# A weighted sum of two experts: the first load takes one token of each partition instead of two

## The chip, the cores and the metric

The kernel runs on one NeuronCore of a Trainium2 chip. The metric is the device time of one execution in microseconds (us). Before the change the median of three runs is 239.23 us (239.12 to 240.39). Times of single instructions and transfers come from one profiled execution of the same kernel.

## The reference

For each of 16 x 1024 tokens there are two expert outputs of 512 float32 values, and two weights. The result is their weighted sum:

```python
batch, seq, hidden, n_experts, k = 16, 1024, 512, 8, 2
expert_outputs: (batch, seq, k, hidden) float32
combine_weights: (batch, seq, k) float32

weights = combine_weights[..., np.newaxis]
return np.sum(expert_outputs * weights, axis=2).astype(np.float32)
```

67.1 MB are read as expert outputs, 0.13 MB as weights, and 33.6 MB are written. No matrix product is in it.

## The kernel before

**Tokens on partitions.** The 16,384 tokens are spread over 128 partitions, 128 tokens each. A token is 4 KB of input (two halves of 512 float32) and 2 KB of output. Of each partition's tokens the first 120 (`main`) are contiguous in memory; the last 8 come from a second region. `rows` (line 40) gives the view for tokens `t` to `t + c` of every partition, so a load of `c` tokens reads 128 contiguous stretches of `c` times 4 KB.

**Tiles and rooms.** A tile is 12 tokens per partition (6 MB in, 3 MB out). There are ten of them and a last one of 8 tokens (`TILES`, line 30). SBUF holds `et`, four rooms of 12 tokens; tile `g` lies in room `g % 4`. All the weights lie in `wt`, 256 values per partition.

**Loads.** `load` (line 68, its transfer on line 71) is issued on SP's queue. Five loads open the kernel (lines 109 to 112): `FIRST` has 2, 10, 12, 12 and 12 tokens, so that the first two fill tile 0 and the others tiles 1 to 3. The very first has the option `max_dma_last_dim`, k x h x 4 = 4096, which cuts its 8 KB rows into 4 KB pieces. No other load has it.

**What else opens.** ACT's queue first gets an 8 KB store of zeros from `zt` into 16 rows of the output (line 104), which later stores overwrite, and then the weights in two transfers (lines 105 and 106, through line 74): 120 tokens' worth, 960 B for each partition, then the last 8, 64 B each. ACT then loads its function table with a small activation (line 107).

**Tiles 0 to 8** (`WHOLE`) are computed on VectorE alone: one multiplication of the room by the weights, broadcast along the 512 values (line 83), and one addition of the two halves (line 90), which puts the result into the room's own first half. **Tile 9** takes 12 ScalarE activations with a scale (line 95) and 12 VectorE instructions that multiply and add (line 96). **Tile 10** (`MIXED`) has its first halves scaled by ScalarE (line 87), its second by VectorE (line 89), and then the addition.

**Stores and reloads** (lines 114 to 124). After each tile its result is stored (line 121), through ACT's queue for tiles 0 to 7. Tiles 8 and 9 are stored together, and tile 10 alone, through SP's. The load of tile `g + 4` is issued on SP after the store of tile `g`, whose room it fills; it waits until that store has landed. The order is written by hand (`manual_schedule`), so each queue runs in the order of these lines.

Of the kernel before, what the change touches and what calls it, by code (L numbers as in the profile page):

```python
# [1 line left out]

# [4 lines left out]


@with_exitstack
def kernel(  # L10
    ctx: ExitStack,
    tc: tile.TileContext,
    expert_outputs: bass.AP,
    combine_weights: bass.AP,
    out: bass.AP,
):

    nc = tc.nc
    b, s, k, h = expert_outputs.shape
    assert k == 2
    n = b * s
    P = nc.NUM_PARTITIONS
    per = n // P
    assert per * P == n

    ROOM, ROOMS = 12, 4
    TILES = [12, 12, 12, 12, 12, 12, 12, 12, 12, 12, 8]  # L30
    FIRST = [2, 10, 12, 12, 12]
    STORES = [[0], [1], [2], [3], [4], [5], [6], [7], [8, 9], [10]]
    WHOLE = [0, 1, 2, 3, 4, 5, 6, 7, 8]
    MIXED = [10]
    LAST = 8
    assert sum(TILES) == per and [g for st in STORES for g in st] == list(range(len(TILES)))
    main = per - LAST
    starts = [sum(TILES[:g]) for g in range(len(TILES))]

    def rows(x):  # L40

        first = x[0 : P * main, :].rearrange("(p t) f -> p t f", p=P)
        second = x[P * main : n, :].rearrange("(p t) f -> p t f", p=P)
        return lambda t, c: first[:, t : t + c, :] if t < main else second[:, t - main : t - main + c, :]

    flat = out.rearrange("b s h -> (b s) h")
    eo = rows(expert_outputs.rearrange("b s k h -> (b s) (k h)"))
    cw = rows(combine_weights.rearrange("b s k -> (b s) k"))
    o = rows(flat)

    dt = mybir.dt.float32
    mult = mybir.AluOpType.mult
    add = mybir.AluOpType.add
    copy = mybir.ActivationFunctionType.Copy

    pool = ctx.enter_context(tc.tile_pool(name="all", bufs=1))
    et = pool.tile([P, ROOMS * ROOM, k * h], dt)
    halves = et.rearrange("p j (k h) -> p (j k) h", k=k)
    wt = pool.tile([P, per * k], dt)
    wk = wt.rearrange("p (t k) -> p t k", k=k)  # L60
    zt = pool.tile([16, 128], dt)
    warm = pool.tile([P, 1], dt)

    def place(t):
        g = max(g for g in range(len(TILES)) if starts[g] <= t)
        return g % ROOMS * ROOM + t - starts[g]

    def load(t, c, **kw):
        at = place(t)
        assert place(t + c - 1) == at + c - 1  # L70
        nc.sync.dma_start(out=et[:, at : at + c], in_=eo(t, c), **kw)  # L71

    def weights(q, t, c):
        q.dma_start(out=wk[:, t : t + c, :], in_=cw(t, c))

    def combine(g, base):
        at, c, t0 = g % ROOMS * ROOM, TILES[g], starts[g]
        if g in WHOLE or g in MIXED:
            room = halves[:, k * at : k * (at + c), :]
            x0, x1 = et[:, at : at + c, 0:h], et[:, at : at + c, h : 2 * h]  # L80
            if g in WHOLE:
                wb = wt[:, k * t0 : k * (t0 + c)].unsqueeze(2).to_broadcast([P, k * c, h])
                nc.vector.tensor_tensor(out=room, in0=room, in1=wb, op=mult)  # L83
            else:
                for i in range(c):
                    x = et[:, at + i, 0:h]
                    nc.scalar.activation(out=x, in_=x, func=copy, scale=wt[:, k * (t0 + i) : k * (t0 + i) + 1])  # L87
                w1 = wk[:, t0 : t0 + c, 1:2].to_broadcast([P, c, h])
                nc.vector.tensor_tensor(out=x1, in0=x1, in1=w1, op=mult)  # L89
            nc.vector.tensor_tensor(out=halves[:, base : base + c, :], in0=x0, in1=x1, op=add)  # L90
            return
        for i in range(c):
            t = k * (t0 + i)
            x0, x1 = halves[:, k * (at + i), :], halves[:, k * (at + i) + 1, :]
            nc.scalar.activation(out=x0, in_=x0, func=copy, scale=wt[:, t : t + 1])  # L95
            nc.vector.scalar_tensor_tensor(  # L96
                out=halves[:, base + i, :], in0=x1, scalar=wt[:, t + 1 : t + 2], in1=x0, op0=mult, op1=add
            )

    with tc.manual_schedule():  # L100
        nc.vector.memset(zt, 0.0)  # L101

        ahead = flat[0 : P * main, :].rearrange("(q t) h -> q (t h)", q=16)
        nc.scalar.dma_start(out=ahead[:, 0:128], in_=zt)  # L104
        weights(nc.scalar, 0, main)
        weights(nc.scalar, main, per - main)
        nc.scalar.activation(out=warm, in_=nc.const_aps.tensor(1.0, (P, 1), dt), func=copy)  # L107

        t = 0
        for i, c in enumerate(FIRST):  # L110
            load(t, c, **({"max_dma_last_dim": k * h * 4} if i == 0 else {}))
            t += c
        assert t == sum(TILES[:ROOMS])
        for j, st in enumerate(STORES):
            base, c = st[0] % ROOMS * ROOM * k, 0
            for g in st:
                combine(g, base + c)
                c += TILES[g]
            assert c <= k * ROOM
            q = nc.sync if j in (8, 9) else nc.scalar  # L120
            q.dma_start(out=o(starts[st[0]], c), in_=halves[:, base : base + c, :])
            for g in st:
                if g + ROOMS < len(TILES):
                    load(starts[g + ROOMS], TILES[g + ROOMS])


# [1 line left out]
_INS = ['expert_outputs', 'combine_weights']  # L128
_OUTS = [((16, 1024, 512), 'float32')]


# [23 lines left out]
```

## Time and profile before

| What | us |
|---|---|
| Median of three runs | 239.23 |
| Lowest, highest | 239.12, 240.39 |
| The profiled execution | 239.0 |
| Its span in the profile | 237.2 |
| VectorE busy in it | 192.3 |
| ScalarE busy in it | 14.0 |
| A multiplication of a whole tile (line 83) | 12.96 |
| An addition of a whole tile (line 90) | 6.56 |

The span runs from the first instruction to the last, and the time around it (1.8 us) is not in the trace. All times within the trace count from the start of the span. SP, ACT and DVE in the rows are SyncE, ScalarE and VectorE; a `q` behind a name (SPq) means the engine's own instruction queue, where transfers are issued and semaphores awaited. `q1` and `q10` are DMA queues; each is served by the same 16 DMA engines. A packet in these rows is one piece that a DMA engine moves. A transfer's landing is the moment at which its semaphore is complete. The page counts 3616 packets, 100.80 MB, and a mean of 425 GB/s over the span.

A row of the waits reads: engine and line that waited, what it waited for, us in total, times, longest wait. A row of DMA issues reads: destination, source, queue, number of such transfers, KB each, median us from issue to landing.

### The profile page before, as it was taken

The page shows a single profiled execution, that of the slowest core. Times are in us where ns is not written, and L with a number is a line of the kernel's source. Part 1 is how long each engine was busy: PE and PEld are TensorE (multiplying, and loading weights), DVE is VectorE, ACT ScalarE, POOL GpSimd, SP SyncE. Part 2 cuts the span into 40 slices and gives each one's busy share as a digit, 9 for nine tenths or more (in the row PEclk, how much of TensorE's full clock was granted, in tenths as well). Part 3 has the DMA queues.
Part 4 walks back from the last instruction along what each step waited for, and adds up shares of the span by engine and source line. Part 5 has one row for each costly group of instructions (what it writes and reads, how often), then busy time and mean ns, then how long its engine had stood idle before and what let it go on. Part 6 is the DMA issues. An engine that isn't in the chain of part 4 may idle for free.

```text
span 237.2 us, 155 instructions
## 1 busy us (share of the span) xinstructions
DVE 192.3 (81%) x33; ACT 14.0 (6%) x22; POOL 0.2 (0%) x4
## 2 busy tenths in 40 slices
DVE  0009999999999999999999879969996998673820
ACT  2000000000000000000000000000000000743400
POOL 0000000000000000000000000000000000000000
DMA  7999999989899999999797999999998979999997
GB/s 289 452 475 398 398 506 423 398 348 514 352 443 423 439 464 464 398 398 522 340 530 340 456 414 448 464 464 398 398 506 356 522 340 464 453 409 442 398 442 309
DMA packets 3616, 100.80 MB, mean 425 GB/s; under 512 B 528, under 2 KB 672, under 8 KB 928
## 3 DMA queue, kind: packets, MB, share of 16 engines
q1 hardware_dynamic: 2144, 75.50, 74.1%
q10 hardware_dynamic: 1472, 25.31, 24.8%
HBM read 67.24 MB, written 33.56 MB: 425 GB/s over the span
## 4 chain that ended last, share of the span: by engine, by line
DMA 58%; DVE 35%; ACT 2%; ACTq 0%; issue 0%; DVEq 0%; SPq 0%
DMA out_dram<-et 29%; DMA et<-in_expert_outputs_dram 22%; DVE et L83 22%; DVE et L90 13%; DMA wt<-in_combine_weights_dram 7%; ACT et L87 2%; ACTq L150 0%; ACTq L104 0%; DVE zt L101 0%; DVEq L83 0%; SPq L71 0%; ACTq L87 0%
## 5 line engine op out<-in xcount | busy, mean ns | idle before, releaser
L83 DVE TENSOR_TENSOR et<-et,wt 128x12288 f32<-128x12288 f32 x9 | 116.6, 12955 | 24.1 <-DMA wt<-in_combine_weights_dram 17.2
L90 DVE TENSOR_TENSOR et<-et 128x6144 f32<-128x6144 f32 (+1 forms) x10 | 63.4, 6345 | 0.9 <-ACT et L87 0.6
L95 ACT ACTIVATE et<-et,wt 128x512 f32<-128x512 f32 x12 | 7.5, 708 | 199.1 <-DMA et<-in_expert_outputs_dram 199.1
L96 DVE SCALAR_TENSOR_TENSOR et<-et,wt 128x512 f32<-128x512 f32 x12 | 8.0, 747 | 3.1 <-ACT et L95 3.1
L89 DVE TENSOR_TENSOR et<-et,wt 128x4096 f32<-128x4096 f32 x1 | 4.4, 4426 | 5.4 <-DMA et<-in_expert_outputs_dram 5.4
L87 ACT ACTIVATE et<-et,wt 128x512 f32<-128x512 f32 x8 | 5.0, 709 | 6.7 <-DMA et<-in_expert_outputs_dram 6.7
L107 ACT ACT_TABLE_LOAD x1 | 1.3, 1283 | 2.4 <-issue 2.4
L101 DVE MEMSET zt<- 16x128 f32 x1 | 0.2, 165 | 0.8 <-PEq L139 0.8
L107 ACT ACTIVATE warm<-const-float32-1.0 128x1 f32<-128x1 f32 x1 | 0.2, 202 | 0.0
L139 POOL MEMSET const-bfloat16-1.0<- 128x1 bf16 x1 | 0.1, 101 | 0.0
L139 POOL MEMSET const-uint8-127<- 128x1 uint8 x1 | 0.1, 101 | 0.0
L139 POOL MEMSET const-float32-0.0<- 128x1 f32 x1 | 0.1, 98 | 0.2 <-issue 0.2
L139 POOL MEMSET const-float32-1.0<- 128x1 f32 x1 | 0.1, 98 | 0.0
## 6 DMA issues: line engine op xcount, KB each, us to landing
et<-in_expert_outputs_dram SPq DMA_DIRECT2D x9, 6144.0 KB, 29.9
out_dram<-et ACTq DMA_DIRECT2D x8, 3072.0 KB, 33.9
out_dram<-et SPq DMA_DIRECT2D x1, 6144.0 KB, 19.8
et<-in_expert_outputs_dram SPq DMA_DIRECT2D x1, 5120.0 KB, 16.7
et<-in_expert_outputs_dram SPq DMA_DIRECT2D x1, 4096.0 KB, 22.4
out_dram<-et SPq DMA_DIRECT2D x1, 2048.0 KB, 9.8
et<-in_expert_outputs_dram SPq DMA_DIRECT2D x1, 1024.0 KB, 4.6
wt<-in_combine_weights_dram ACTq DMA_DIRECT2D x1, 120.0 KB, 16.7
```

Source lines behind the costliest of these rows:

```text
L83: nc.vector.tensor_tensor(out=room, in0=room, in1=wb, op=mult)
L87: nc.scalar.activation(out=x, in_=x, func=copy, scale=wt[:, k * (t0 + i) : k * (t0 + i) + 1])
L89: nc.vector.tensor_tensor(out=x1, in0=x1, in1=w1, op=mult)
L90: nc.vector.tensor_tensor(out=halves[:, base : base + c, :], in0=x0, in1=x1, op=add)
L95: nc.scalar.activation(out=x0, in_=x0, func=copy, scale=wt[:, t : t + 1])
L96: nc.vector.scalar_tensor_tensor(out=halves[:, base + i, :], in0=x1, scalar=wt[:, t + 1 : t + 2], in1=x0, op0=mult, op1=add)
L101: nc.vector.memset(zt, 0.0)
L107: nc.scalar.activation(out=warm, in_=nc.const_aps.tensor(1.0, (P, 1), dt), func=copy)
L139: nc = _bacc.Bacc("TRN2", target_bir_lowering=False, num_devices=1)
```

## The change

The sizes of the opening loads go from 2, 10, 12, 12, 12 to 1, 11, 12, 12, 12 tokens per partition. The first DMA then loads one token per partition, a 4 KB row, and keeps its option; the second loads the other 11 tokens of tile 0, 44 KB rows. Besides, the rooms' size becomes a list with one entry for each room, all 12, and a room's place is looked up in a list of starts. The places come out as before, and so do all other instructions.

```diff
-    ROOM, ROOMS = 12, 4
+    ROOM = [12, 12, 12, 12]
+    ROOMS = len(ROOM)
+    SITE = [sum(ROOM[:i]) for i in range(ROOMS)]
     TILES = [12, 12, 12, 12, 12, 12, 12, 12, 12, 12, 8]
-    FIRST = [2, 10, 12, 12, 12]
+    FIRST = [1, 11, 12, 12, 12]
...
+    assert all(c <= ROOM[g % ROOMS] for g, c in enumerate(TILES))
...
-    et = pool.tile([P, ROOMS * ROOM, k * h], dt)
+    et = pool.tile([P, sum(ROOM), k * h], dt)
...
     def place(t):
         g = max(g for g in range(len(TILES)) if starts[g] <= t)
-        return g % ROOMS * ROOM + t - starts[g]
+        return SITE[g % ROOMS] + t - starts[g]
...
     def combine(g, base):
-        at, c, t0 = g % ROOMS * ROOM, TILES[g], starts[g]
+        at, c, t0 = SITE[g % ROOMS], TILES[g], starts[g]
...
-            base, c = st[0] % ROOMS * ROOM * k, 0
+            base, c = SITE[st[0] % ROOMS] * k, 0
...
-            assert c <= k * ROOM
+            assert c <= k * ROOM[st[0] % ROOMS]
```

## The prediction

> **What bounds the kernel now.** I read the page's DMA rows first, then the chain of waits, then the DMA queues in short windows. The page gives VectorE 81% of the span, but the queue rows decide:
>
> ```profile
> q1 hardware_dynamic: 2144, 75.50, 74.1%
> q10 hardware_dynamic: 1472, 25.31, 24.8%
> ```
>
> These are packets, MB and share of the 16 DMA engines' span; q1 carries what SP issues, q10 what ACT issues. Together 98.9%: the engines idle 1.1% of 237.2 us, 2.6 us. A window from 1.8 to 236.0 us gives
>
> ```profile
> q1 hardware_dynamic: 2141, 75.50, 75.0%
> q10 hardware_dynamic: 1472, 25.31, 25.2%
> ```
>
> 100.2%, so the idle time is 1.8 us before the first packet and about 1 us behind the last. The kernel moves its 100.8 MB without a gap. The chain of waits (start, duration, what) says where work begins and ends:
>
> ```profile
> 1.42 16.66 DMA wt<-in_combine_weights_dram
> ...
> 18.17 12.97 DVE et L83
> ...
> 76.67 30.88 DMA out_dram<-et
> ...
> 107.62 29.94 DMA et<-in_expert_outputs_dram
> ...
> 222.21 4.43 DVE et L90
> ```
>
> VectorE starts at 18.17, when the weights land. From there the chain goes through long DMA pieces: 29.94 us for a 6 MB load and 30.88 us for a 3 MB store. These are queueing: a load and a store together (9.44 MB) take 21.75 us, the spacing of load issues (64.09, 85.89, 107.62), which is 434 GB/s. VectorE needs only 12.96 + 6.56 = 19.5 us for a tile, so from the sixth tile on it waits for loads:
>
> ```profile
> DVE et L83 <- DMA wt<-in_combine_weights_dram: 17.2, 1, 17.2
> DVE et L83 <- DMA et<-in_expert_outputs_dram: 6.9, 4, 2.2
> ```
>
> **The start, packet by packet.** The DMA issue rows (KB, us from issue to landing):
>
> ```profile
> et<-in_expert_outputs_dram SPq DMA_DIRECT2D x1, 5120.0 KB, 16.7
> et<-in_expert_outputs_dram SPq DMA_DIRECT2D x1, 1024.0 KB, 4.6
> wt<-in_combine_weights_dram ACTq DMA_DIRECT2D x1, 120.0 KB, 16.7
> wt<-in_combine_weights_dram ACTq DMA_DIRECT2D x1, 8.0 KB, 30.8
> ```
>
> The first load is issued at 0.73 and lands at 5.3. The second, issued at 1.21, lands at 17.9. The 120 KB of weights, issued at 1.42, land at 18.08. The packet count says how rows travel: q1's 2144 packets are 256 of 4 KB (the first load), 13 x 128 for the other 11 loads and two stores, one per partition, and 16 closing ones for each of 14 transfers (224). So the second load is 128 packets of 40 KB, 8 per engine; the weights are 8 per engine of 960 B. Two short windows, 6 to 7 and 14 to 15 us, show them alternating, one for one:
>
> ```profile
> q1 hardware_dynamic: 16, 0.66, 151.4%
> q10 hardware_dynamic: 16, 0.02, 4.4%
> ```
>
> The same two lines come from both windows. Each weights packet waits for one big packet, so the eight of them end with the second load's eighth. The small weights transfer repeats it: it lands at 32.7 with the third load (32.5), 8 rounds in 14.6 us, 1.83 us a round.
>
> **The change part by part.**
>
> *Issue.* SP's first issue takes 0.43 us (256 packets), the others 0.33. With 128 packets I take 0.33: the second load's issue moves from 1.21 to about 1.1. Whether the first packet comes sooner is not shown; bounds 0 and -0.1 us; I take -0.05. All later issues in the opening move by as much and queue behind loads in transit. The fifth load, issued at 5.34 when the first landed (4.94 us of SP issues from 0.73 on), is issued at about 4.0; it has two loads ahead of it: nothing.
>
> *Transfer of tile 0.* Bytes are equal. A window from 3.2 to 3.6 us shows 40 packets of 4 KB, 0.16 MB, so 0.16 us per packet and engine. Ten tokens in 40 KB are one round of (17.9 - 5.3)/8 = 1.57 us, 0.157 per token. 128 packets dropped are 8 per engine: 8 x 0.16 = 1.28 us less, and eight rounds longer by 0.157 are 1.26 more: -0.02 us. The first packets are slower: 1 MB took from 1.8 to 4.8, 3.0 us against 16 x 0.16 = 2.6. If those 0.4 us go with the packets, half is saved (-0.2); if they belong to starting, nothing. I take -0.05, since later small packets show no such cost.
>
> *Does the second load follow in time?* The first load's packets now end at 4.8 - 1.3 = 3.5 us. The second was ready at 4.8 at the latest and is issued 0.1 earlier, so at worst the engines idle 4.7 - 3.5 = 1.2 us. SP's first load needed 1.1 us from issue to packet; that gives 1.1 + 1.1 = 2.2, no gap. I take 0, the row of the same queue, and keep 0 to +1.2.
>
> *The weights.* The page's 8 KB store of zt goes ahead of them on ACT's queue. Its packets move in the window 3.6 to 4.4, between 4 KB packets where a turn costs 0.16 us. Now only 44 KB packets are there from 3.5 on, so its data, its closing packet, and then the weights, each wait for one: a round of 11 x 0.157 = 1.73 us. The eight weights packets then need more rounds than the second load has left and end beside the third, at 1.83 us a round. If zt still slips in before 3.5, the weights lose one round; behind the first big packet, two; behind the second, three. Bounds: 0 rounds and 4 (7.3 us). I take two, +3.7 us: the weights land near 21.8 and VectorE starts there instead of at 18.17. Queued behind that wait on VectorE are all tiles, and on ACT the stores of their results.
>
> *Who pays for that?* Nobody, as long as a packet is queued. While the first store is late by 3.7 us, q1 has loads to move (four loads, 24 MB, 58 us at 434 GB/s), and moves them without sharing. Store 0 is issued at 37.75 + 3.7 = 41.4, lands near 67.8, and load 4 is issued then instead of at 64.09. Load 3 landed at 5.34 + 66.9 = 72.2; it now gains the two 24 KB packets that did not come between, 2 x 0.91 = 1.8 us (24 KB at 434/16 GB/s), and lands near 70.4: load 4 is still queued in time. From then on loads land some 1.8 us earlier, so the 6.9 us of waits in the row above shrink and VectorE has made up its 3.7 us by about tile 7 (21.75 - 19.5 = 2.2 us a tile). The cover is the DMA backlog; without it the whole 3.7 us would show. At the end the last store, issued at 226.7, lands 9.8 us later although 2 MB need 4.8: it stands behind the 6 MB store on q1, with some 5 us to spare less its own start. Nothing at the end is late.
>
> Sum: -0.05 - 0.02 - 0.05 + 0 + 0 = -0.1 us, on a profiled 239.0 (span 237.2 and 1.8 around it). The three runs have a median of 239.23, 0.2 above, so I forecast 239.1.
>
> **The rivals.**
>
> *A gap behind the short first load* (above): up to +1.2 us, middle 0.6, so 239.8 and at most 240.4. For it: zt's store needed over 2.5 us from issue (1.01) to its first packets. Against it: SP's own 1.1 us, and 4 KB packets followed at once by big ones. The Trainium skill, "DMA: Bandwidth & Descriptors", section "Rules for kernel authors", asks for at least 1 MiB per DMA, and its "Anatomy of one DMA" gives a fixed 2.0 us and bytes at 436 GB/s for transfers issued from GpSimd; the halved first load lasts 1.2 us by that, which would leave 0.8 us uncovered, an estimate from that page, 239.9. The trace shows no transfer from GpSimd, so it can neither agree nor disagree here.
>
> *The weights ride with the third load altogether*: slower. The small weights transfer did so, landing at 32.7. VectorE would start at 32.8, 14.6 us late. Loads 0 to 3 alone land at 17.9 + 3 x 14.6 = 61.7, and store 0's 3 MB need 7.3 us of the engines: they are done at 69.0, whenever store 0 began. Store 1 is issued 19.6 + 19.5 us after VectorE's start (37.75 and 57.2 against 18.17). So the engines run dry once VectorE starts after 69 - 39 = 30 us, 12 us or 6 to 7 rounds late. Then load 4 starts 0.5 us of landing (last 4 KB packets 4.8, landed 5.3) and 1.1 us of issue later: +1.6 us, 240.7, and 242.3 if it recurs with load 5; I take 241.5. Against: two to four rounds are what the turn-taking gives.
>
> *The end is set by latencies, not by the engines*: faster. The chain ends in load 10, VectorE, last store; if its loads land 1.8 us earlier and the stores follow, 239.2 - 1.8 = 237.4. Against: the engines are full until 236, and no bytes go away.
>
> *The weights lose no round* (zt is served at once): 239.1 as well, by the same backlog; only VectorE's start differs.
>
> **How the numbers follow.** Forecast 0.62; no round lost 0.08; gap 0.12; late weights 0.12; latency end 0.06. One of the three runs shown stands 0.5% above the others (240.39), so about 0.5% is what a measurement can tell from no change. A quarter of the gap's chance reaches that (0.03), and I leave 0.03 of the forecast for such a spread on the slow side and 0.01 on the fast side. Faster 0.07; slower 0.12 + 0.03 + 0.03 = 0.18; same 0.75. The low end is the forecast with every small gain (-0.1 and -0.2 in place of -0.1 in sum) and a little spread, 238.5; the high end holds the gap's 240.4 and some of the spread, 240.7. Late weights (but for their lower end) and the latency end stay outside, with 0.18.
>
> **What would show it.** q1 2016 packets instead of 2144, 128 of them of 4 KB. The second load lands near 17.9. The weights land at 20 to 25 and VectorE's first multiplication starts there; its waits for loads shrink from 6.9 us. q1 and q10 together near 99% of the span. Wrong: a stretch with no packets near 3.5 us or near 69 us, or weights landing after 30 us.

## The result and the profile after

The changed kernel takes 239.64 us (median of 22 runs, 239.34 to 240.21) and the kernel before 239.06 (22 runs beside them). The ratio is 1.002, with a 95% interval of 1.001 to 1.0029: slower by 0.6 us. The forecast was 239.1, a tenth faster. The profiled execution took 239.72 us with a span of 237.9, 0.72 more than before.

The queue rows of the page after (packets, MB, share of 16 engines' span). In such a row for a short window, a packet counts where it starts, and with its full time, so that a share can pass 100%:

```profile
q1 hardware_dynamic: 2016, 75.50, 74.1%
q10 hardware_dynamic: 1472, 25.31, 24.8%
```

128 packets fewer, as foreseen, and the same bytes. The shares are those of before, of a span that is 0.3% longer: the engines are as full as before, so the packets themselves must take longer. The DMA issue rows after (KB, us to landing):

```profile
et<-in_expert_outputs_dram SPq DMA_DIRECT2D x1, 5632.0 KB, 16.7
...
et<-in_expert_outputs_dram SPq DMA_DIRECT2D x1, 512.0 KB, 3.5
wt<-in_combine_weights_dram ACTq DMA_DIRECT2D x1, 120.0 KB, 18.1
```

and the start of the chain of waits after (start, duration, what):

```profile
1.47 18.09 DMA wt<-in_combine_weights_dram
...
19.64 12.97 DVE et L86
```

Tile 0's data are there as early as before; the weights land at 19.56 instead of 18.08, and VectorE starts 1.47 us later. A window of the DMA queues after, from 5.1 to 5.6 us, when the engines take the second 44 KB packet of the second load, shows why:

```profile
q1 hardware_dynamic: 16, 0.72, 333.0%
q10 hardware_dynamic: 11, 0.01, 6.0%
```

All 16 engines start a big packet, but only 11 weights packets have gone ahead. Five engines missed their turn, and their closing packet of the weights comes behind the third load's first packet, 1.8 us later. The weights count as landed only after the last of the 16 closing packets. In the kernel before, the same moment (6.2 to 6.7 us) has 16 and 16.

**Where the 0.7 us come in.** From 17 to 36 us the loads' packets of both kernels run alike. They part where store 0, the first big store, meets the loads. Before, from 43 to 44 us:

```profile
q10 hardware_dynamic: 16, 0.39, 91.2%
```

After, the same window, and then 45.5 to 47 us:

```profile
q10 hardware_dynamic: 13, 0.32, 74.1%
q1 hardware_dynamic: 2, 0.10, 28.8%
...
q10 hardware_dynamic: 16, 0.39, 60.8%
```

Before, all 16 engines take their first 24 KB packet of the store between 43.2 and 43.6 us. After, 13 do; the other three start another 48 KB load packet and take the store's first one a round later (45.8 to 46.3); a round is one load packet on each of the 16 engines. The later of the two windows holds those three packets and 13 second ones. The 48 KB packets around it are long. A share times the window's length gives their mean where each of the 16 engines starts one. Before, windows 36 to 38, 40 to 42 and 46.5 to 47.5 us:

```profile
q1 hardware_dynamic: 16, 0.79, 90.9%
...
q1 hardware_dynamic: 16, 0.79, 116.1%
...
q1 hardware_dynamic: 16, 0.79, 206.2%
```

1.82, 2.32 and 2.06 us: a 48 KB packet takes 1.82 us, except for two rounds at the store's start. After, windows 40 to 42 and 43.4 to 45 us:

```profile
q1 hardware_dynamic: 16, 0.79, 123.4%
...
q1 hardware_dynamic: 16, 0.79, 144.7%
```

2.47 and 2.32 us. The two long rounds are 0.15 and 0.26 us longer than the two before, 0.4 us on the mean of the engines. From 236.2 us to the end the trace before has no packet at all on either queue; after, it has these:

```profile
q1 hardware_dynamic: 15, 0.02, 2.6%
```

The last engines end 0.7 us later than before, the mean one 0.4 us; the other 0.3 is spread between the engines. The place of the loss can be read from all the packets of both traces, if one in transit is counted by the part of its time that has passed, and bytes are turned into time at 434 GB/s: the changed kernel is 0.01 us behind the kernel before at 40 us, 0.41 at 50, and 0.42 at 235.5. What is lost between 40 and 50 us is never made up, and nothing more is lost.

### The profile page after: what moved, and what is told of

Read it like the earlier page. It is cut to its first block, busy times and chain, and to the rows that moved or that the text cites. A ratio compares the mean times of both kernels' runs of the same rounds, so it can differ in the third digit from the quotient of the medians.

```text
span 237.9 us, 155 instructions
## 1 busy us (share of the span) xinstructions
DVE 192.2 (81%) x33; ACT 13.9 (6%) x22; POOL 0.2 (0%) x4
## 4 chain that ended last, share of the span: by engine, by line
DVE 45%; DMA 45%; issue 3%; ACT 2%; ACTq 0%; DVEq 0%; SPq 0%
DVE et L86 32%; DMA et<-in_expert_outputs_dram 20%; DMA out_dram<-et 17%; DVE et L93 13%; DMA wt<-in_combine_weights_dram 8%; ACT et L90 2%; ACTq L153 0%; ACTq L107 0%; DVE zt L104 0%; DVEq L86 0%; SPq L74 0%; ACTq L90 0%
## 6 DMA issues: line engine op xcount, KB each, us to landing
et<-in_expert_outputs_dram SPq DMA_DIRECT2D x1, 5632.0 KB, 16.7
```

## The experiments

The first four runs put two theories against each other: L, that the time goes with the later first store; S, that it goes with the one-token load itself. In all of them the only spare work is VectorE multiplications into a scratch tile that nothing reads.

**One token, weights ahead of the store of zeros.**

```diff
-        nc.scalar.dma_start(out=ahead[:, 0:128], in_=zt)
         weights(nc.scalar, 0, main)
+        nc.scalar.dma_start(out=ahead[:, 0:128], in_=zt)
```

> The changed kernel with the weights issued on ACT's queue ahead of the 8 KB store of zeros. Theory L (late first store: the 0.6 us come because VectorE starts 1.5 us later and the first store goes out 1.5 us later): the weights land before the second load, VectorE starts near 18.0, the first store is issued near 37.6, time 239.0 to 239.2, ratio to the kernel before 1.000. Theory S (the shape of the first load itself costs it, by the way it sets the 16 engines off): VectorE starts at 18.0 as well, but the time stays at 239.6, ratio 1.002.

Measured: 239.23 us, ratio 1.0006 (0.9992 to 1.0021). VectorE starts at 18.48, the first store is issued at 38.07. That is nearly L's number, and not S's 239.6.

**Two tokens, the same edit.**

> The kernel before (two tokens, then ten) with the weights ahead of the store of zeros: the control for the run above. Theories L and S alike: VectorE starts near 18.0, first store near 37.6, time 239.0 to 239.2. If it differs from the kernel before by more than 0.3 us, the order of the two transfers has an effect of its own.

Measured: 239.15 us, ratio 1.0013 (0.9994 to 1.0033); seven runs lie at 239.0 to 239.2 and five at 240.1 to 240.5, so the median says little of the second group.

**Two tokens, VectorE delayed.**

```diff
+        for m in [680, 680]:
+            nc.vector.tensor_tensor(out=spare[:, 0:m], in0=et[:, 10, 0:m], in1=et[:, 11, 0:m], op=mult)
         for j, st in enumerate(STORES):
```

> The kernel before (two tokens, then ten), with two spare VectorE multiplications of 680 elements, some 1.5 us together, ahead of tile 0; they write a scratch tile that nothing reads. First store issued near 39.2, as in the changed kernel. Theory L: time 239.5 to 239.8, ratio 1.002, and the 48 KB packets around 40 to 46 us stretched as in the changed kernel. Theory S: 239.0 to 239.2.

Measured: 239.8 us, ratio 1.0025 (1.0013 to 1.0037), no run under 239.63. The first store is issued at 39.56; two engines take it at 43.3 and 14 at 45.1 to 45.5 (windows from 43 to 44 and 45 to 45.5 us):

```profile
q10 hardware_dynamic: 2, 0.05, 11.4%
...
q10 hardware_dynamic: 14, 0.34, 159.6%
```

The opening loads are those of the kernel before, and the loss is there: a late first store is enough.

**One token, weights ahead, VectorE delayed.**

> The changed kernel with the weights ahead of the zeros and the same two spare multiplications: first store near 39.1. Theory L: 239.5 to 239.8. Theory S: 239.6 too. With the first run it tells whether the one-token load has any part in it: L wants a difference of 0.5 us between the two, S none.

Measured: 240.02 us, ratio 1.0026 (1.0008 to 1.0043). L's numbers for the four are met to 0.3 us; S's for the first and the third are not. For this last run that is partly luck: in its trace all 16 engines take the store between 45.1 and 46.1 us, and the mean engine ends at 236.0 (235.9 in the kernel before). Its last engine ends at 237.4, so its loss is all spread, of the kind described below at 0.3 us of delay. The first run's 239.23 and this 240.02 also lie above their two-token partners, by 0.1 and 0.2.

What the third run and the change have in common is not lateness alone, but that the store arrives while the engines change packets. So the next theory was P, phase (the loss depends on where the store falls between two changes of packets, and comes back with every round), against R, a rate per microsecond of lateness.

**Two tokens, weights ahead, three delays** (one spare multiplication of 310 elements, one of 690, three of 565).

> Two tokens first, weights ahead of the zeros, one spare VectorE multiplication of 310 elements (about 0.5 us; scratch only): first store issued near 38.3 us. Theory P (phase: a store's packets can be taken some 1.6 us after its issue; where that moment falls into the 0.4 us in which the 16 DMA engines change from one 48 KB packet to the next, some engines take the store a round of 1.8 us later than the others, and they stay out of step): available at 39.9, the engines change at 39.0 to 39.4 and 40.8 to 41.2, so all take it together: 239.0 to 239.2. Theory R (every microsecond that VectorE starts later costs 0.35 to 0.4 us): 239.25.

Measured: 239.03 us (238.93 to 239.14), ratio 0.9989 (0.9974 to 1.0005). Store issued at 38.11, all engines together.

> The same with one spare multiplication of 690 elements (about 0.9 us): first store issued near 38.7, available at 40.3, between two changes. Theory P: 239.0 to 239.2. Theory R: 239.4.

Measured: 239.47 us, ratio 1.0004 (0.9986 to 1.0022). P missed: four runs at 239.0 to 239.1, eight at 239.46 to 239.78. The profiled one is of the four (239.08, store issued at 38.64, all engines together).

> The same with three spare multiplications of 565 elements (about 2.3 us): first store issued near 40.1, available at 41.7, after the change at 40.8 to 41.2 and before that at 42.6 to 43.0; all engines take it together, one round later than in the kernel before. Theory P: 239.0 to 239.3 and the engines' first 24 KB packets within 0.6 us of each other, near 45.2. Theory R: 239.9 to 240.0.

Measured: 239.12 us, ratio 1.0001 (0.9992 to 1.0009). Store issued at 40.09; all engines take it at 45.2 to 45.5 (window from 45 to 45.5 us):

```profile
q10 hardware_dynamic: 16, 0.39, 182.4%
```

VectorE starts 2.34 us later than in the kernel before, and next to nothing is lost (0.07 us). R falls.

**The changed kernel, delayed.** The first attempt put the spare multiplication on tile 0's data.

> The changed kernel (one token first, zeros ahead of the weights) with one spare multiplication of 600 elements (about 0.8 us) ahead of tile 0: first store issued near 40.0, available at 41.6, between two changes. Theory P: faster than the changed kernel although VectorE starts later: 239.0 to 239.3. Theory R: 239.9 to 240.0.

Measured: 239.75 us, ratio 1.0026 (1.0012 to 1.0039). It missed because the edit did nothing: the spare work (17.99 to 18.77 us) lay inside the wait for the weights, and the store was still issued at 39.17. Eleven engines took it in one round and five in the next. It repeats the changed kernel, with a wider spread (238.84 to 240.27). The next one waits for the weights:

```diff
+        for m in [240, 240]:
+            nc.vector.tensor_tensor(out=spare[:, 0:m], in0=et[:, 10, 0:m], in1=wt[:, 0:m], op=mult)
         for j, st in enumerate(STORES):
```

> The changed kernel with two spare VectorE multiplications of 240 elements (0.4 us each; scratch only) that wait for the weights, so that they do delay tile 0: first store issued near 40.1 us, 0.85 later than in the changed kernel. Theory P (phase; store taken some 1.6 us after issue, engines change packets at about 39.0, 40.8 and 42.6 us, each change spread over 0.4 to 0.5 us): 41.7 lies between two changes, 239.0 to 239.4, faster than the changed kernel though it starts later. Theory R (each us of delay costs 0.35 to 0.4): 239.9 to 240.0.

Measured: 239.04 us (nine of 12 runs at 238.86 to 239.12, three at 239.5 to 241.2), ratio 1.001 (0.9996 to 1.0025). Two rows of its timeline (start, duration), and the window from 45 to 46 us:

```profile
20.52 12.96 DVE L87 TENSOR_TENSOR et<-et,wt 128x12288 f32<-128x12288 f32 x1
...
40.10 0.35 ACTq L127 DMA_DIRECT2D out_dram<-et  x1
```

```profile
q10 hardware_dynamic: 16, 0.39, 91.2%
q1 hardware_dynamic: 6, 0.29, 73.6%
```

VectorE starts 0.9 us later than in the changed kernel, all 16 engines take the store in one round, and the profiled execution takes 238.86 us, span 237.1: 0.8 less.

**One token, weights ahead, 0.3 us of delay** (150 elements).

> One token first, weights ahead of the zeros, one spare multiplication of 150 elements (0.3 us): first store issued near 38.2. Theory P, and with it that the one-token load costs nothing by itself: 239.0 to 239.15, as the two-token kernel with 0.5 us of wait. If the one-token load has a part of its own (its engines start further apart): 239.2 to 239.4. Theory R: 239.35.

Measured: 239.97 us (238.95 to 240.9), ratio 1.003 (1.001 to 1.005): a miss for both; four runs lie at 238.95 to 239.12, where P had it, and eight at 239.55 to 240.9. Its trace, which is of the eight, has one long round at the store's start (2.36 us) and all engines in the same round, but they are apart from the opening on. Windows from 5.6 to 6.1 and 6.1 to 6.6 us, when they take their second 44 KB packet:

```profile
q1 hardware_dynamic: 11, 0.50, 228.9%
...
q1 hardware_dynamic: 4, 0.18, 83.2%
```

The 16 starts lie 0.92 us apart at the first big packet (3.94 to 4.86), against 0.24 in the kernel before and 0.41 in the changed one, and the last engine ends 1.5 us behind the first (237.2 and 235.7), while the mean one ends at 236.0 (235.9 in the kernel before). With the weights ahead, their packets alternate with the 4 KB packets of the short first load; that some engines come out late for this reason is likely, but not shown. The two earlier runs of this kind have 0.71 and 0.78.

**Two tokens, a delay that reaches the next change of packets** (four of 550 elements).

> Two tokens first, weights ahead of the zeros, four spare multiplications of 550 elements (3.1 to 3.2 us): first store issued near 41.0, one round of 1.82 us after the place where the changed kernel issues it. Theory P: split again, 239.4 to 239.8, slower than with 2.3 us of wait. Theory R: 240.2 to 240.3. A flat 239.1 would speak against both.

Measured: 239.88 us, ratio 1.0039 (1.0027 to 1.0051), nearer to P. Store issued at 40.82; 14 engines take it in one round, two a round later.

**One token, tile 2's load in packets of half the size.**

```diff
-            load(t, c, **({"max_dma_last_dim": k * h * 4} if i == 0 else {}))
+            load(t, c, **({"max_dma_last_dim": k * h * 4} if i == 0 else {"max_dma_last_dim": 24576} if i == 3 else {}))
```

> The changed kernel with the load of tile 2, which is in transit when the first store starts, cut into 24 KB packets instead of 48 KB: the engines then change every 0.9 us, and an engine that misses the store waits 0.9 us, not 1.8. Theory P: the loss is about halved, 239.2 to 239.4. Theory R: unchanged, 239.6, since VectorE starts as late as in the changed kernel.

Measured: 239.33 us (239.08 to 239.7), ratio 1.0013 (1.0004 to 1.0021), with the store issued at 39.20 as in the changed kernel. Half the loss, as P had it.

**The changed kernel beside itself with two delays** (240, 240 and 100 elements; four of 240).

> The changed kernel itself, beside the next two. Both theories: 239.5 to 239.8, first store issued near 39.2, the engines' first 24 KB packets split over two rounds.

Measured: 239.76 us, ratio 1.0033 (1.0021 to 1.0045); eight engines in one round and eight in the next.

> The changed kernel with about 1.1 us of spare VectorE multiplications that wait for the weights (240, 240 and 100 elements; scratch only): first store issued near 40.3. Theory P: between two changes of packets, 239.0 to 239.2. Theory R (each us of delay costs 0.35 to 0.4): 240.0.

Measured: 239.61 us (238.91 to 240.12), ratio 1.0017 (1.0004 to 1.003). Four of 12 runs lie at or below P's 239.2, the profiled one among them (238.97; store issued at 40.34, all engines together); the other eight lie at 239.45 to 240.1. R's 240.0 is not the middle either: one kernel gives both 238.9 and 240.1, though when its store was issued is known for the profiled run alone.

> The changed kernel with about 1.7 us of spare multiplications (four of 240 elements): first store issued near 41.0, a round of 1.82 us behind the changed kernel's. Theory P: split again, 239.4 to 239.9, slower than with 1.1 us. Theory R: 240.2 to 240.3.

Measured: 239.91 us, ratio 1.0038 (1.0025 to 1.0051). Store issued at 40.92; ten engines take it in one round and six in the next:

```profile
q10 hardware_dynamic: 10, 0.25, 81.4%
...
q10 hardware_dynamic: 6, 0.15, 42.8%
```

(windows 44.8 to 45.5 and 47.8 to 48.6 us). Slow, mixed, slow, where R wants a steady rise to 240.2. The time itself lies between P's range (up to 239.9) and R's (from 240.2); what speaks against R are the 239.04 us above, at 0.85 us of delay, and the traces.

The profiled executions in order of the first store's issue, without the three whose engines came apart in the opening (one token, weights ahead) and the one with half packets:

| Store 0 issued, us | Engines per round | Profiled, us | Kernel |
|---|---|---|---|
| 37.75 | 16 | 239.0 | before |
| 37.81 | 16 | 239.07 | two tokens, weights ahead |
| 38.11 | 16 | 238.97 | the same, wait 0.5 |
| 38.64 | 16 | 239.08 | the same, wait 0.9 |
| 39.17 | 11, 5 | 239.69 | one token, wait without effect |
| 39.23 | 13, 3 | 239.72 | the changed kernel |
| 39.27 | 8, 8 | 239.74 | the changed kernel again |
| 39.56 | 2, 14 | 239.94 | two tokens, wait 1.5 |
| 40.09 | 16 | 239.01 | two tokens, weights ahead, wait 2.3 |
| 40.10 | 16 | 238.86 | one token, wait 0.85 |
| 40.34 | 16 | 238.97 | one token, wait 1.1 |
| 40.82 | 14, 2 | 239.72 | two tokens, weights ahead, wait 3.2 |
| 40.92 | 10, 6 | 240.19 | one token, wait 1.7 |

Every execution of the table with one round is at 238.9 to 239.1, every one with two at 239.7 or more, and the order along the first column is fast, slow, fast, slow, which fits the 1.82 us of a 48 KB packet as a period: the slow rows at 39.2 to 39.6 and 40.8 to 40.9 lie 1.3 to 1.8 us apart. One round alone does not make a run fast: the three left out took the store in one round too, within 0.7 to 1.0 us, and took 239.26, 240.1 and 240.3 us. Their engines had come apart before; that this is the whole reason is not shown.

## Why the prediction was wrong

**Issue.** Right in size. The first issue takes 0.38 us instead of 0.43, and the first packet comes 0.07 us earlier; -0.05 was taken. That the other issues take 0.33 was misread: in the opening of the kernel before, the next three take 0.4 to 0.6, and the second load's issue moved only from 1.21 to 1.17.

**Transfer of tile 0.** Right: the second load lands 16.7 us after its issue in both kernels, and the engines' shares are unchanged.

**A gap behind the first load.** Right that there is none: the 44 KB packets begin at 3.5 to 3.9 us, as the 4 KB ones end. The 0.8 us uncovered, an estimate from the fixed cost in the Trainium skill ("DMA: Bandwidth & Descriptors", "Anatomy of one DMA"), did not show on this path.

**The weights.** The mechanism was right and the size too large: one round on five engines, 1.48 us, in place of two rounds and 3.7. The zeros' packets still went through at 3.5 to 3.9 us, ahead of the first 44 KB packets; for that case the prediction had one round lost, and 11 engines did not lose even that. The Trainium skill, on the same page in "Queues, rings and completion order", has each engine go round its queues a packet at a time. The windows agree, with one row as the packet (40 to 48 KB on one queue, 960 B on the other), not the 9 to 17 descriptors that the page calls typical.

**"Who pays for that? Nobody, as long as a packet is queued."** This is the step that failed. The engines did stay full, and the forecast stopped there: it counted a full engine as one that moves bytes at 434 GB/s. At a store's start it is full and slower (2.3 to 2.5 us for a 48 KB packet in place of 1.82), and how much slower depends on whether the 16 engines take the store in the same round. The term was put at 0 and measures +0.6 to +0.7 us. The table shows that the store's moment decides, not its lateness: 0.9 us later still, the changed kernel is back at 239.04. The gain of 1.8 us for the loads did not come in full: VectorE's waits for loads shrank from 6.9 us to 5.9, but 13 engines took the late store at the very moment they took the early one (43.3 us), since they take it only at a change of packets, so the loads got nearly no time alone. Three engines were a round later, the store landed 2.5 us late, and load 4 was issued at 66.61 instead of 64.09.

**The rivals.** None of the four came: no gap, no weights beside the whole third load (VectorE at 19.64, not 32.8), no earlier end, no weights without a lost round. The direction of slower was given 0.18, to a size above 0.5%; the true size, 0.2%, lay in the range but on the other side of the forecast.

**What stays open.** Why the packets grow at a store's start, and why most of the added length falls into the second round, is not shown. Nor is what lengthens single runs by more: the kernel before has four of 35 runs at 240.1 to 240.9 beside the first experiments and six of 33 beside the next, two tokens with the weights ahead has five of 12, and none of these was profiled. The runs fix the bad moments only roughly: issues at 37.75 to 38.1 and 40.1 us are good, 39.2 to 39.6 and 40.8 to 40.9 bad. At 38.64 and 40.34 runs of one kernel come out both ways, which P as put, with one change of 0.4 us, did not foresee. Of the runs without a profile the split is inferred from their times. No version beat the kernel before: the best, two tokens with the weights ahead and 0.5 us of wait, has 239.03 us against 239.05 beside it.

## What to carry to other kernels

When DMA engines are full from end to end, a delay elsewhere can still cost: ask not only whether a packet is queued, but when the next queue's first packets arrive and whether all engines take them in the same round. With rows of 48 KB a round is 1.8 us, so a shift of a microsecond in a start-up can cost 0.6 us at the end, and a further one can win it back; in the one run that tried smaller packets where the two streams meet, they halved the loss. Before a small loss is put down to the edited line, shift the suspected event alone, by less and by more than a round: a rate rises, a phase comes back.

## What the runs showed of the hardware

A store issued into an empty queue waited 5.4 us for its first packet (37.75 to 43.2 us), behind one packet in transit and two more of 1.8 to 2.4 us. Engines that started apart ended apart: 0.92 us between the 16 first big packets at 4 us was 1.5 us between the ends at 236 us, in a run 1.1 us slower than the kernel before.
